# One kernel, one change: the head's order of work, and where three modulation rows are computed

## The chip, the cores and the metric

The kernel runs on one core of a Trainium2 chip. A core has TensorE (matrix products, PE in the profile; PEld is its loading of stationary operands), VectorE (DVE), ScalarE (ACT), GpSimd (POOL) and SyncE (SP), which here does nothing but issue transfers between the chip's memory and the core's. The metric is the device time of one execution in microseconds (us).

## What is computed

One layer of a hybrid backbone on 1024 tokens of 1024 features, in float32, with 256 context tokens beside them. Cut to what matters here:

```python
sh1, sc1, g1, sh2, sc2, g2 = adaln(c, ada_w, ada_b)       # silu(c) @ ada_w + ada_b, 6 rows of 1024
csh1, csc1, *_ = adaln(c_ctx, ada_w, ada_b)
h_ctx = modulate(ctx, csh1, csc1)                         # standardize(.) * (1 + scale) + shift
k_ctx, v_ctx = context_kv(h_ctx, w_in)
h = modulate(x, sh1, sc1)
u_hy, q, k, v, gates = split(h @ w_in)
y_hy = hyena_branch(u_hy)                                 # short convolution, then a long one
y_at = latent_attention(q, k, v, cos, sin, k_ctx, v_ctx, sinks)
x = layer_norm(ALPHA * x + g1 * mix(y_hy, y_at, gates))
x = layer_norm(ALPHA * x + g2 * hier_moe(modulate(x, sh2, sc2)))
```

## The kernel before

Every large product is made exact by splitting both factors into a high and a low part (`split`, lines 250 to 254: ScalarE rounds the high part, VectorE subtracts) and adding three products (`mm3`, lines 256 to 260).

**The head** is `phase_start`, with the queues' order written out by hand: inside `tc.manual_schedule()` the order of the program is the order on each engine. The modulation of x (shift and scale) is computed in four quarters of 256 features. `fetch(q)` (line 365) loads 2 MB of `ada_w` in two transfers into one of three `aw` buffers; `part(q)` (line 377) multiplies it with the silu of both conditions in 16 products; ScalarE copies the result to `mrow`; `turned(q)` (line 387) turns it into columns by 8 small products, and VectorE adds the bias into `ad`. `load(t)` (line 373) loads 128 tokens of x; `stat_a` and `stat_b` (lines 398 to 420) standardize them, even tiles by VectorE's statistics, odd ones by ScalarE's. `turn(q, g)` (line 457) transposes two blocks of 128 features of 512 tokens (g is the half) on TensorE and returns `then`, which applies scale and shift and splits the result into `hT` (`mod_split`, line 548: ScalarE and VectorE) and puts the two blocks on the list `todo`. `kv(n)` (line 445) takes n items off that list; each is six products, three into keys and three into values. `later` holds the weights of keys and values (`wri`, `wv`), loaded early and split at `run(x)`. Last come the context's statistics, `context(k)` for four pairs of blocks, and the context's keys and values; `self.ahead()` (line 608) then loads and splits the first weights of the queries. There are two split weight buffers (`whi`, `wli`) and one raw one (`wri`).

Before the change, the statistics of x0 to x3 come ahead of `part(0)`; then follow turn(0, 0), the splits of `later`, the statistics of x4 to x7, and from there on quarter after quarter.

**The query stage** is `phase_qkv`. Keys are rotated and split, values turned, then `queries()` projects four chunks of queries (48 products each) and rotates, scales and splits them on VectorE and ScalarE. Outside the hand-written part a planner orders each engine's queue by its own estimate of when an instruction can start, in the order of the program where several can. `weave(...)` (line 200) interleaves generators in proportion to given counts. Here it weaves the queries with `mod_rows` (line 690) for `MOD_Q`, three half rows of the later modulation (g1, sh2): each is cleared on POOL, gets its bias by a transfer, then adds 8 loads of 128 x 512 weights (256 KB, buffers `mr`, the tile `aw` in the profile) by one VectorE operation each into `ac`, sums over the partitions by a product with ones (`p1`, the tile `p`), is copied by ScalarE and stored to `d_row`. These rows are read only much later.

**The attention stage** is `phase_att`: it weaves `attend` (66 steps, 32 blocks of scores and values) with `conv_all` (96 steps: twelve projections of 48 products for the short convolution).

Of the kernel before, what the change touches and what calls it, by code (L numbers as in the profile page):

```python
# [18 lines left out]
P = 128  # L19
# [225 lines left out]
class K:  # L245
# [106 lines left out]
    def phase_start(self):  # L352

        tc, nc, A = self.tc, self.nc, self.A
        with ExitStack() as es:
# [10 lines left out]
            def fetch(i):  # L366
                w = aw[i] = sb.tile([P, 8, 512], F32, name=f"aw{i}", tag="aw", bufs=3)
                for j in range(2):
                    c0 = j * 1024 + i * 256
                    nc.sync.dma_start(w[:, :, j * 256:(j + 1) * 256],  # L370
                                      A["ada_w"][:, c0:c0 + 256].rearrange("(k p) c -> p k c", p=P))
# [5 lines left out]
            def part(i):  # L377

                pm[i] = ps.tile([P, 512], F32, name="pm", tag="pm", bufs=1)
                for r in range(2):  # L380
                    for j in range(4):
                        k = 4 * r + j
                        nc.tensor.matmul(pm[i][32 * j:32 * j + 32], s2[:, k], aw[i][:, k], start=(r == 0), stop=(r == 1))
                mrow[i] = sb.tile([P, 512], F32, name="mrow", tag="mrow", bufs=2)
                nc.scalar.activation(mrow[i], pm.pop(i), AF.Copy)
# [69 lines left out]
            def turn(q, g):  # L455

                pt = [block(k, g) for k in (2 * q, 2 * q + 1)]

                def then():
                    for k in range(2):  # L460
                        out(2 * q + k, g, pt[k])
                        todo.append((2 * q + k, g))
                return then

            with tc.manual_schedule():
                for t in range(4):
                    load(t)
                fetch(0)
                wv, jk = (self.kvp.tile([P, 1280], F32, name=n, tag="kvb") for n in ("wv", "jk"))
                jk = jk[:, :1024]  # L470
                later = [self.ahead(True), self.ahead(True, wv)]
                for t in range(4, 8):
                    load(t)
                for i in range(1, 3):
                    fetch(i)
                nc.vector.memset(s2, 0.0)
                nc.scalar.activation(s2[:, :, :2], cols[:, :16].rearrange("p (k c) -> p k c", c=2), AF.Silu)
                warm = sb.tile([P, 1], F32, name="warm", bufs=1)
                nc.scalar.activation(warm, self.eps, AF.Sqrt)
                nc.vector.tensor_copy(silc, s2[:, :, 0])  # L480
                for c in range(2):
                    nc.vector.tensor_copy(bias[:, :8, c], cols[:, 16:24])
                    nc.vector.tensor_scalar(bias[:, 8:, c], cols[:, 24:32], 1.0, None, op0=OP.add)
                stat_a(xn[0], 0)
                stat_a(xn[1], 1)
                stat_b(xn[0], 0)
                stat_a(xn[2], 2)
                stat_b(xn[1], 1)
                stat_a(xn[3], 3)
                stat_b(xn[2], 2)  # L490
                stat_b(xn[3], 3)
                part(0)
                fetch(3)
                turned(0)
                turn(0, 0)()
                for x in later:
                    run(x)
                    w.append(self.w_ready.pop(0))
                stat_a(xn[4], 4)
                stat_a(xn[5], 5)  # L500
                stat_b(xn[4], 4)
                stat_a(xn[6], 6)
                stat_b(xn[5], 5)
                stat_a(xn[7], 7)
                stat_b(xn[6], 6)
                stat_b(xn[7], 7)
                kv(2)
                turn(0, 1)()
                for q in range(1, 4):
                    kv(1)  # L510
                    part(q)
                    if q == 1:
                        cx = sb.tile([P, 8, 512], F32, name="cx", tag="aw", bufs=3)
                        for t in range(2):
                            cn[t] = cx[:, 2 * t:2 * t + 2].rearrange("p a b -> p (a b)")
                            nc.sync.dma_start(cn[t], A["ctx"][t * P:(t + 1) * P])
                    kv(1)
                    turned(q)
                    then = turn(q, 0)
                    if q > 1:  # L520
                        kv(1)
                    then()
                    if q == 3:
                        for t in range(2):
                            stat_a(cn[t], t, cx[:, 4:6].rearrange("p a b -> p (a b)"))
                            stat_b(cn[t], t)
                    if q > 1:
                        kv(1)
                    turn(q, 1)()
                kv(2)  # L530
                context(0)
                kv(2)
                context(1)
                kb, vb = (self.kvp.tile([P, 1280], F32, name=n, tag="kvb") for n in ("kb", "vb"))
                for g in range(2):
                    for j, b in enumerate((kb, vb)):
                        nc.scalar.activation(b[:, g * 512:(g + 1) * 512], acc[j, g], AF.Copy)
                    context(2 + g)
            for j, b in enumerate((kb, vb)):
                pc = self.pjp.tile([P, 512], F32, name="pjc", tag="pj", bufs=4)  # L540
                for k in range(KD):
                    self.mm3(pc[:, :256], w[j][0][:, k], w[j][1][:, k], self.cT[0][k // 2][:, k % 2],
                             self.cT[1][k // 2][:, k % 2], k == 0, k == KD - 1)
                nc.scalar.activation(b[:, 1024:], pc[:, :256], AF.Copy)
                if j == 0:
                    self.ahead()
            return kb, vb

    def mod_split(self, sb, pt, ad, k, c, hi, lo):
# [89 lines left out]
    def phase_qkv(self, cps, kb, vb):  # L639
        tc, nc, A = self.tc, self.nc, self.A  # L640
        with ExitStack() as es:
# [43 lines left out]
                        nc.vector.scalar_tensor_tensor(q[oth], qb[own], 0.125, q[own].bitcast(F32), op0=OP.mult,  # L685
                                                       op1=OP.subtract)

            T2 = lambda n: sb.tile([P, 2, 256], F32, name=n, tag="mr", bufs=5)
            weave((queries(), 32), (self.mod_rows(self.pjp, T2, dict(tag="pj", bufs=4), MOD_Q), 1 + 9 * len(MOD_Q)))

    def mod_rows(self, pp, T2, ptag, parts):

# [55 lines left out]
    def phase_att(self):  # L748
        tc, nc, A = self.tc, self.nc, self.A
        with ExitStack() as es:  # L750
            sb = es.enter_context(tc.tile_pool(name="at_sb", bufs=2, reuse_waits="tile"))
            pp = es.enter_context(tc.tile_pool(name="at_ps", bufs=2, space=PSUM, reuse_waits="tile"))
            mk = sb.tile([P, 1920], BF16, name="mk", bufs=1)
            nc.gpsimd.dma_start(mk, A["k_mask"])

            def fill():
                yield from self.conv_all(pp, sb)

            weave((self.attend(pp, sb, mk), 66), (fill(), 96))

    def attend(self, pp, sb, mk):
        nc = self.nc
# [1043 lines left out]
```

## Time and profile before

| | us |
|---|---|
| median of 3 runs | 1266.92 |
| lowest, highest | 1261.25, 1267.8 |
| the profiled execution | 1266.46 |
| its span in the trace | 1264.9 |

The profile is of one execution. All later rows and times within it are counted from the start of its span, and 1.56 us of its time lie outside the span. Busy time is the time in which an engine executes an instruction that counts as work; a row of a timeline gives start, duration, engine, line and operation, the tile written and the tiles read, a count where equal neighbours are merged, and in brackets how long the engine had been idle and what it waited for.

### The profile page before, as it was taken

Reading aid. Unit: us, or ns where it says so; the run is one execution under the profiler, and the core shown is the slowest. Engines: PE = TensorE matmul, PEld = TensorE weight load, DVE = VectorE, ACT = ScalarE, POOL = GpSimd, SP = SyncE. Lnnn points to the kernel's source line nnn. Section 1 sums busy time; section 2 is a strip of 40 time slices with the busy share of each in tenths; the row PEclk is TensorE's granted clock in tenths of the full one; section 3 lists DMA queues with packets and bytes.
Section 4 is the critical chain, followed back from the end, with each engine's and each line's share of the span. In section 5 each row is a group of like instructions: output and inputs, shape, how many; then the busy total and the mean of one; then the engine's idle time right before and its main releaser. Section 6 shows DMA issues by size and latency. Waiting matters only on the chain. (4 is left out here: it accounts for less than half of the span.)

```text
span 1264.9 us, 16231 instructions
## 1 busy us (share of the span) xinstructions
PE 1122.6 (89%) x5640; PEld 901.4 (71%) x5640; DVE 925.7 (73%) x1715; ACT 600.0 (47%) x1023; POOL 149.1 (12%) x159
## 2 busy tenths in 40 slices
PE   3788799999999999998998879899977999999970
PEld 2576588888887777876887757678854777778850
DVE  4459779888887357896778777756875788878827
ACT  4464366665556444443344324323443656555505
POOL 0000000000000012122010000000313332233220
PEclk9899899999999999999998999989978999999995
DMA  9424321111111545545855588743395999999726
GB/s 330 158 71 146 102 50 63 42 59 43 59 42 62 173 158 166 171 135 179 286 154 161 164 290 280 241 156 117 80 176 205 346 335 306 300 310 320 213 42 266
DMA packets 78088, 220.07 MB, mean 174 GB/s; under 512 B 9911, under 2 KB 22839, under 8 KB 71477
## 3 DMA queue, kind: packets, MB, share of 16 engines
q1 hardware_dynamic: 64933, 180.66, 42.5%
q0 software_dynamic: 12640, 38.15, 11.2%
q8 instruction: 45, 0.74, 0.2%
q14 instruction: 38, 0.31, 0.1%
q10 hardware_dynamic: 432, 0.21, 0.1%
HBM read 178.41 MB, written 45.78 MB: 177 GB/s over the span
## 5 line engine op out<-in xcount | busy, mean ns | idle before, releaser
L258 PE MATMUL pj<-hT,whi 128*128 128x512 f32 x512 | 209.8, 410 | 4.5 <-ACT o L723 2.3
L260 PE MATMUL pj<-hT,wli 128*128 128x512 f32 x512 | 203.3, 398 | 1.6 <-DVE wli L254 1.6
L259 PE MATMUL pj<-hT,whi 128*128 128x512 f32 x512 | 204.4, 399 | 0.0
L253 ACT ACTIVATE eh<-er 128x1024 fp32r<-128x1024 f32 x96 | 99.3, 1058 | 57.9 <-PE pg L260 22.9
L254 DVE TENSOR_TENSOR el<-er,eh 128x1024 fp32r<-128x1024 f32 x96 | 113.8, 1218 | 13.7 <-ACT eh L253 13.4
L258 PEld LDWEIGHTS pj<-hT,whi 128*128 128x128 f32 x512 | 97.4, 190 | 29.2 <-issue 7.2
L260 PEld LDWEIGHTS pj<-hT,wli 128*128 128x128 f32 x512 | 97.3, 190 | 21.3 <-DVE wli L254 2.3
L259 PEld LDWEIGHTS pj<-hT,whi 128*128 128x128 f32 x512 | 97.3, 190 | 19.1 <-issue 3.4
L258 PE MATMUL pg<-eh,xh 128*128 128x512 f32 x200 | 81.1, 406 | 0.0
L259 PE MATMUL pg<-el,xh 128*128 128x512 f32 x200 | 79.3, 397 | 0.0
L260 PE MATMUL pg<-eh,xl 128*128 128x512 f32 x200 | 79.2, 396 | 0.0
L819 ACT ACTIVATE th<-pt 128x512 fp32r<-128x512 f32 (+1 forms) x88 | 44.2, 536 | 41.5 <-PE pt L815 39.6
L1545 POOL DMA_INDIRECT d_r<-y,idi x25 | 45.7, 1828 | 142.6 <-DVE y L1696 40.9
L702 DVE SCALAR_TENSOR_TENSOR ac<-aw,silc,ac 128x512 f32<-128x512 f32 x48 | 36.2, 757 | 35.5 <-DMA aw<-ada_w 35.1
L788 DVE CUSTOM_DVE_ANT_0 p<-sp,mk,srow 128x640 f32<-128x640 f32 (+1 forms) x64 | 52.8, 845 | 8.0 <-PE sp L777 6.6
L793 ACT ACTIVATE p<-p,m 128x640 f32<-128x640 f32 (+1 forms) x64 | 50.8, 797 | 15.9 <-DVE m L790 15.9
L820 DVE TENSOR_TENSOR tl<-pt,th 128x512 fp32r<-128x512 f32 (+1 forms) x88 | 52.4, 611 | 7.5 <-ACT th L819 7.4
L258 PE MATMUL po<-wo,mg 128*128 128x512 f32 x128 | 52.6, 411 | 5.4 <-DVE gt L1225 3.1
L253 ACT ACTIVATE whi<-wri 128x1024 fp32r<-128x1024 f32 x33 | 35.0, 1061 | 44.9 <-PE pj L259 32.2
L260 PE MATMUL po<-wo,mg 128*128 128x512 f32 x128 | 52.1, 407 | 0.0
L259 PE MATMUL po<-wo,mg 128*128 128x512 f32 x128 | 52.1, 407 | 0.0
L254 DVE TENSOR_TENSOR wli<-wri,whi 128x1024 fp32r<-128x1024 f32 x33 | 40.3, 1220 | 15.7 <-ACT whi L253 15.5
(476 smaller groups left out, 2768.2 us busy)
## 6 DMA issues: line engine op xcount, KB each, us to landing
er<-w_gu SPq DMA_DIRECT2D x32, 1024.0 KB, 8.3
wri<-w_in SPq DMA_DIRECT2D x33, 512.0 KB, 3.7
er<-w_dn SPq DMA_DIRECT2D x16, 1024.0 KB, 8.3
aw<-ada_w SPq DMA_DIRECT2D x48, 256.0 KB, 4.2
x<-x SPq DMA_DIRECT2D x16, 512.0 KB, 8.8
aw<-ada_w SPq DMA_DIRECT2D x8, 1024.0 KB, 12.0
d_gate<-go SPq DMA_DIRECT2D x32, 256.0 KB, 2.4
gt<-d_gate SPq DMA_DIRECT2D x32, 256.0 KB, 4.1
```

The costliest lines, as they stand in the source:

```text
L253: a = self.nc.scalar.activation(hi, src, AF.Copy)
L254: return a, self.nc.vector.tensor_sub(lo, src, hi.bitcast(F32))
L258: mm(ps, whi, xhi, start=first, stop=False)
L259: mm(ps, whi, xlo, start=False, stop=False)
L260: mm(ps, wlo, xhi, start=False, stop=last)
L702: nc.vector.scalar_tensor_tensor(acc, w, self.silc[:, k:k + 1], acc, op0=OP.mult, op1=OP.add)
L788: nc.vector.tensor_tensor_reduce(p[:, a, :T], src, mk[:, o:o + T], 1.0, self.sink[:, h0 + a:h0 + a + 1], OP.add, OP.max, m[:, a:a + 1])
L793: nc.scalar.activation(p[:, a, :T], p[:, a, :T], AF.Exp, bias=m[:, 2 + a:3 + a], accum_out=m[:, 6 + a:7 + a])
L819: nc.scalar.activation(th[:, :N], pt[:, :N], AF.Copy)
L820: nc.vector.tensor_sub(tl[:, :N], pt[:, :N], th[:, :N].bitcast(F32))
L1545: self.nc.gpsimd.indirect_dma_start(out=self.d_r, out_offset=bass.IndirectOffsetOnAxis(ap=idx, axis=0), in_=y, in_offset=None, bounds_chec ...
```

## The change

In the head, `fetch(0)` goes ahead of the first four loads of x, and `fetch(1)` between the key and value weights and the other four. `part(0)` and `turned(0)` come ahead of all statistics. The first half of the tokens (g = 0) goes through the quarters 0 and 1 before the statistics of the second half, with the splits of `later` and items of `kv` put between `turn` and `then`; afterwards the halves follow in another order, the context's statistics come behind the last `turn`, and the first weights of the queries are asked for right after the context's load. `mod_rows` for `MOD_Q` leaves the weave with the queries and joins the one of the attention, with three `mr` buffers in place of five and two `pj` banks in place of four.

```diff
             with tc.manual_schedule():
+                fetch(0)
                 for t in range(4):
                     load(t)
-                fetch(0)
                 wv, jk = (self.kvp.tile([P, 1280], F32, name=n, tag="kvb") for n in ("wv", "jk"))
                 jk = jk[:, :1024]
                 later = [self.ahead(True), self.ahead(True, wv)]
+                fetch(1)
                 for t in range(4, 8):
                     load(t)
-                for i in range(1, 3):
-                    fetch(i)
+                fetch(2)
...
+                part(0)
+                fetch(3)
+                turned(0)
                 stat_a(xn[0], 0)
                 stat_a(xn[1], 1)
...
-                part(0)
-                fetch(3)
-                turned(0)
-                turn(0, 0)()
-                for x in later:
-                    run(x)
-                    w.append(self.w_ready.pop(0))
+                then = turn(0, 0)
+                run(later[0])
+                w.append(self.w_ready.pop(0))
+                then()
+                run(later[1])
+                w.append(self.w_ready.pop(0))
+                part(1)
+                cx = sb.tile([P, 8, 512], F32, name="cx", tag="aw", bufs=3)
+                for t in range(2):
+                    cn[t] = cx[:, 2 * t:2 * t + 2].rearrange("p a b -> p (a b)")
+                    nc.sync.dma_start(cn[t], A["ctx"][t * P:(t + 1) * P])
+                wq = self.ahead(True)
+                kv(1)
+                turned(1)
+                then = turn(1, 0)
+                kv(1)
+                then()
                 stat_a(xn[4], 4)
...
                 kv(2)
                 turn(0, 1)()
-                for q in range(1, 4):
-                    kv(1)
-                    part(q)
-                    if q == 1:
...
-                    kv(1)
-                    turned(q)
-                    then = turn(q, 0)
-                    if q > 1:
-                        kv(1)
-                    then()
-                    if q == 3:
-                        for t in range(2):
-                            stat_a(cn[t], t, cx[:, 4:6].rearrange("p a b -> p (a b)"))
-                            stat_b(cn[t], t)
-                    if q > 1:
-                        kv(1)
-                    turn(q, 1)()
+                part(2)
+                turn(1, 1)()
+                kv(2)
+                turned(2)
+                turn(2, 0)()
+                kv(2)
+                turn(2, 1)()
+                kv(2)
+                part(3)
+                kv(1)
+                turned(3)
+                turn(3, 0)()
+                kv(1)
+                turn(3, 1)()
+                for t in range(2):
+                    stat_a(cn[t], t, cx[:, 4:6].rearrange("p a b -> p (a b)"))
+                    stat_b(cn[t], t)
                 kv(2)
                 context(0)
...
                 if j == 0:
-                    self.ahead()
+                    run(wq)
...
-            T2 = lambda n: sb.tile([P, 2, 256], F32, name=n, tag="mr", bufs=5)
-            weave((queries(), 32), (self.mod_rows(self.pjp, T2, dict(tag="pj", bufs=4), MOD_Q), 1 + 9 * len(MOD_Q)))
+            run(queries())
...
-            weave((self.attend(pp, sb, mk), 66), (fill(), 96))
+            T2 = lambda n: sb.tile([P, 2, 256], F32, name=n, tag="mr", bufs=3)
+            weave((self.attend(pp, sb, mk), 66), (fill(), 96),
+                  (self.mod_rows(pp, T2, dict(tag="pj", bufs=2), MOD_Q), 1 + 9 * len(MOD_Q)))
```

## Rows read from the trace of the kernel before

**Rows 1.** The page, part 1: busy time, share of the span, instructions.
```profile
PE 1122.6 (89%) x5640; PEld 901.4 (71%) x5640; DVE 925.7 (73%) x1715; ACT 600.0 (47%) x1023; POOL 149.1 (12%) x159
```

**Rows 2.** Windows by stage: stretch, its length, busy per engine, PEclk, DMA share, GB/s.
```profile
53.00:84.00 31.00, 27.47 (x164) 20.16 (x162) 14.72 (x32) 16.73 (x29) 0.52 (x1) 1.00 0.00 1
...
91.00:135.00 44.00, 32.81 (x132) 23.97 (x130) 42.15 (x46) 17.87 (x23) 1.05 (x2) 0.92 0.48 150
135.00:165.00 30.00, 28.59 (x118) 21.88 (x118) 21.22 (x23) 9.09 (x11) 0.73 (x1) 0.94 0.36 101
165.00:410.00 245.00, 240.95 (x1406) 204.67 (x1405) 206.54 (x513) 154.40 (x342) 2.24 (x25) 1.00 0.16 50
```

**Rows 3.** Windows of 2 us in the head, the same columns.
```profile
40.00:42.00 2.00, 1.32 (x5) 0.48 (x3) 0.81 (x2) 1.83 (x3) 0.00 (x0) 0.50 1.10 367
...
46.00:48.00 2.00, 2.00 (x16) 0.93 (x9) 0.00 (x0) 0.60 (x1) 0.00 (x0) 0.93 0.00 0
```

**Rows 4.** Timeline of SP in the head: start, duration, what is issued.
```profile
11.27 1.87 SPq L375 DMA_DIRECT2D x<-x  x4
...
33.76 2.87 SPq L598 DMA_DIRECT2D wri<-w_in  x1
47.27 0.82 SPq L516 DMA_DIRECT2D cx<-ctx  x2
```

**Rows 5.** Timeline of the head, all engines: statistics, first part, column, transposes.
```profile
8.73 1.28 DVE L411 BATCH_NORM_STATS2 bs<-x 128x6 f32<-128x512 f32 x2
...
16.81 3.64 PE L383 MATMUL pm<-aw,s 128*32 128x512 f32 x16 [16.81 <-DMA aw<-ada_w]
...
23.06 0.23 DVE L396 TENSOR_TENSOR ad<-pc,adb 128x4 f32<-128x4 f32 x2 [4.69 <-PE pc L393]
...
29.51 1.28 DVE L411 BATCH_NORM_STATS2 bs<-x 128x6 f32<-128x512 f32 x2
...
38.33 0.81 DVE L420 TENSOR_SCALAR x<-x,va 128x1024 f32<-128x1024 f32 x1
...
39.20 1.33 PE L425 MATMUL pt<-small,x 128*128 128x128 f32 x5 [1.25 <-DVE x L420]
...
44.37 2.83 PE L383 MATMUL pm<-aw,s 128*32 128x512 f32 x16
```

**Rows 6.** Timeline of TensorE in the head: products of 512 columns.
```profile
30.38 0.63 PE L258 MATMUL kv<-hT,whi 128*128 128x512 f32 x1
...
60.03 0.39 PE L258 MATMUL kv<-hT,whi 128*128 128x512 f32 x1
60.26 0.40 PE L259 MATMUL kv<-hT,whi 128*128 128x512 f32 x1
```

**Rows 7.** Timeline: the context's statistics and transposes, the first query product.
```profile
72.55 1.28 DVE L411 BATCH_NORM_STATS2 bs<-cx 128x6 f32<-128x512 f32 x2
...
78.61 0.66 PE L437 MATMUL pt<-small,cx 128*128 128x128 f32 x4 [2.53 <-ACT hT L557]
...
91.36 0.49 PE L258 MATMUL pj<-hT,whi 128*128 128x512 f32 x1
```

**Rows 8.** Timeline of the query stage: TensorE's waits, a VectorE addition.
```profile
107.26 0.50 PE L260 MATMUL pj<-hT,wli 128*128 128x512 f32 x1 [1.59 <-DVE wli L254]
...
115.19 1.02 PE L705 MATMUL p<-ac,onec 128*1 128x512 f32 x2 [1.07 <-DVE ac L702]
...
133.05 2.20 DVE L702 SCALAR_TENSOR_TENSOR ac<-aw,silc,ac 128x512 f32<-128x512 f32 x3
...
133.90 1.86 PE L705 MATMUL p<-ac,onec 128*1 128x512 f32 x2 [6.55 <-issue]
```

**Rows 9.** Groups, 91 to 156 us: count, busy, mean ns, idle before.
```profile
L702 DVE SCALAR_TENSOR_TENSOR ac<-aw,silc,ac 128x512 f32<-128x512 f32 x24 | 17.8, 751 | 5.3 <-DMA aw<-ada_w 4.8
...
L705 PE MATMUL p<-ac,onec 128*1 128x512 f32 x6 | 3.9, 738 | 7.6 <-issue 6.5 <-DVE ac L702 1.1
```

**Rows 10.** Waits, 165 to 412 us: who waited for whom, us, times, longest.
```profile
DVE m L795 <- ACT m L794: 12.3, 13, 1.8
```

More of the change, by code (lines that the diff above doesn't have):

```diff
@@ L508, in phase_start @@
                 turn(0, 1)()
-                for q in range(1, 4):
-                    kv(1)
-                    part(q)
-                    if q == 1:
-                        cx = sb.tile([P, 8, 512], F32, name="cx", tag="aw", bufs=3)
-                        for t in range(2):
-                            cn[t] = cx[:, 2 * t:2 * t + 2].rearrange("p a b -> p (a b)")
-                            nc.sync.dma_start(cn[t], A["ctx"][t * P:(t + 1) * P])
-                    kv(1)
-                    turned(q)
-                    then = turn(q, 0)
-                    if q > 1:
-                        kv(1)
-                    then()
-                    if q == 3:
-                        for t in range(2):
-                            stat_a(cn[t], t, cx[:, 4:6].rearrange("p a b -> p (a b)"))
-                            stat_b(cn[t], t)
-                    if q > 1:
-                        kv(1)
-                    turn(q, 1)()
+                part(2)
[15 more added lines that the diff above has]
+                    stat_b(cn[t], t)
                 kv(2)
```

## The prediction, made before the changed kernel was run

> **What bounds the kernel now.** I read the page's first part, then the table by stage, then the order of time in the head. Over the span TensorE is busy 89% and VectorE 73% [rows 1], but that is a mean over stages with different limits. [Rows 2] are the stages that the change touches. The **head** (0 to 91 us) is first bound by transfers: the DMA share is 1.10 up to about 42 us, and at 46 nothing flows [rows 3]. After that TensorE works through what is left, 27.5 of 31 us busy. In the **query stage** (91 to 156) VectorE is the bound: 42.15 of 44 us busy, TensorE only 32.8. The **attention stage** (165 to 410) is TensorE's: 240.95 of 245 us, VectorE 206.5. So the order of the head decides when the queries start (91.36, [rows 7]), VectorE decides how long they take, and what is added to the attention is paid where TensorE or VectorE has no room.
>
> The clock has two levels: a product of 512 columns takes 0.63 us early and 0.39 later, when the next starts 0.23 us on [rows 6]. I call 0.23 the high rate and 0.43 the low one. TensorE's whole head, counted in high-rate work, is about 48 us.
>
> **The head, first half.** Engines run their queues in program order here. Evidence: VectorE stands idle for 4.69 us ahead of the modulation column at 23.06, and only afterwards begins x4 at 29.51 [rows 5], though x4 to x7 were issued from 11.27 on [rows 4]. So I play the new order with old durations.
>
> (a) The weights fetch(0) go ahead of x0 to x3. Before, part(0) began at 16.81 [rows 5] with 4.4 MB landed, half of it x. With that half behind it, from the first bytes at about 2 us, I estimate 9.4 plus 1.5 for what is in flight beside it: 11. The column `ad` came 6.25 us after part(0) began and takes 0.3: 17.5.
>
> (b) turned(0) now stands before the statistics on VectorE. They began at 8.73 and now wait for `ad`: 17.5, or 8.8 later, although x0 is there at about 12.5. The chain took 9.6 us, so x3 is ready at 27.2 and the first transposes end at 28.4, as 39.20 + 1.33 follows x7 [rows 5].
>
> (c) TensorE goes on, where it used to wait: part(1) 2.83 [rows 5], one kv item of six products 2.6 at the low rate, turned(1) 1.0, turn(1,0) 1.2, another kv item. ScalarE and VectorE finish turn(1,0)'s output at 38.5, and only then, in program order, come the statistics of x4 to x7. They took 9.6 us from 29.51 (x7 ends at 38.33 + 0.81, [rows 5]); now 38.5 to 48.1, so 9.0 later. In exchange TensorE has done 6.5 us of high-rate work by then that used to follow (part(1) 1.9, turned(1) and turn(1,0) 0.95 each, two kv items 2.7). Balance: +2.5.
>
> **The head, second half.** From the end of turn(0,1)'s transposes (39.20 + 1.33 = 40.5, [rows 5]) to the queries took 50.9 us for 40.9 us of work; 10 were lost to the low rate, which ended shortly after 46 [rows 3], and to waits. Now 34.4 us of work start at 49.4. Low rate until about 55: 2.5 us, since TensorE idles from 41 to 48 as it did from 33 to 41. After that a kv pair (2.7 us) stands beside every output of ScalarE (2.1 us), so the small waits go. One wait grows. The context's statistics come behind turn(3,1). Their chain took 5.7 us (72.55 to 78.3; transposes at 78.61, [rows 7]); it would begin at about 74.3, and only one kv pair, ending at 75.0, covers it. TensorE idles 5 us instead of 2.5. From the context's transposes on it is 12.75 us as before (78.61 to 91.36), 2.4 of them lost. Sum: 49.4 + 34.4 + 2.5 + 5 + 2.4 = 93.7 against 91.36, about **+2**. Bounds: -4, if the weights land at 9.5 and the high rate is kept; +6, if the clock falls in both new gaps.
>
> That gap of 5 us has two nearest rows: one of 2.5 us (76.1 to 78.6) left the rate high, one of 6.55 us ahead of 133.90 left the next products low [rows 8]. I charge nothing for it in the sum and 2.4 us (12 products at 0.43 for 0.23) in the upper bound. The Trainium skill (TensorE: Matmul & The Clock Gate, "HAM oscillation — how this bites in real kernels") speaks against such gaps: an array left waiting is throttled again and starts each burst cold. By that rule the head would be +4.4 instead of +2, and the time 1262.4.
>
> The early request for Q's weights I cost at nothing: the third `wri` was already issued at 33.76 [rows 4], and its split waits for a free weight buffer at 90.07, which the change leaves where it is. Without that cover it would be one transfer, 3.5 us. The context's load, at 47.27 before, moves to about 42, with 30 us to spare [rows 4].
>
> **The query stage loses the three rows.** That removes 24 VectorE operations, 17.8 us [rows 9], the 24 loads of 256 KB between Q's weight loads on SP, and three products `p1`. `p1` cost 3.9 us busy and 7.6 idle on TensorE [rows 9], most of it one wait: 6.55 us ahead of 133.90, where the last addition on VectorE started at 133.05 [rows 8]. After it six products ran at the low rate: 1.2 us. The stall at the second chunk stays: 107.26 waits for `wli`, which stands behind the four `kk` operations on VectorE; three additions (2.2 us) stood ahead of those, but ScalarE's `kk` and `whi` end late as well, so only 0.8 goes. Sum 3.9 + 7.6 + 1.2 + 0.8 = **-13.5**. Then TensorE's 192 products at 0.23 are the bound and VectorE, with about 9 us a chunk against 10.9, keeps up. Bounds: -9, if part of the additions is issued ahead into this stage (its buffers are free then); -17, if the `kk` stall goes as well.
>
> **The attention stage gets them.** TensorE: three `p1` of 1.02 us [rows 8] in a stage that is 98% busy: 3.1. `p1` takes one of two `pj` banks, so the next group of the convolution waits for the copy-out of the last (two ScalarE operations, about 1.4 us) unless attention products stand between: 0.5 each, 1.5. VectorE: 18 us more on 206.5 gives 225 of 245. It now waits 12.3 us for ScalarE's sums alone [rows 10], and additions are ready at any time, so they fall into such holes: 0.4. Queued behind an addition that waits for its load are scores and values, and TensorE after them; with three `mr` buffers, one the sum, two loads are ahead, at a step of 9 us against some 4 to land. Of the rows' other steps POOL's three clearings of the sum take 0.53 us each, on an engine that does nothing there but clear two columns a chunk. On SP a load that waits for a buffer holds back `d_at` and the next weights, which have 4 us to spare. Sum **+5**. Bounds: 0 (the 4 us that TensorE idles cover it; less is excluded, since work is added to the bound) and +21 (18 + 3.1, nothing hidden).
>
> The rest, from 410 us on, has the same instructions and moves as a whole. +2 - 13.5 + 5 = -6.5 on the profiled execution's 1266.46 gives **1260.0**; the median of 1266.92 is 0.46 above that, inside the spread of the three runs.
>
> **Rivals.**
> 1. *The rows slip back.* Their buffers lie outside the query stage's, so the planner may start them there. Then part of VectorE's load stays: query stage -6, attention +2, head +2: 1264.5. For it: other steps far down the program are already issued early. Against: `p1` has no bank before the attention, so at most one row can be finished. Chance 0.18.
> 2. *The head gains.* Statistics of x4 to x7 begin when x has landed, near 30, not at 38.5, because columns or outputs come sooner than I play them. Then the 6.5 us that were done ahead count in full and the queries start near 85: 1251.5. Against: the idle VectorE at 18.4 to 23 [rows 5]. Chance 0.18.
> 3. *Slower: VectorE becomes the attention's bound.* Convolution tails come in bursts there (two operations of 1.28 us and a split of 1.22 in one step); with an addition on top, VectorE lags and TensorE waits at every one. Price up to 21 us: 1276. The balance tips when the attention pays 11.5, slower by 0.5% from 18. Against: 20 us of VectorE still free. Chance 0.12.
> 4. *The clock falls.* The context's gap of 5 us ends at the low rate, and the 12 products behind it cost 2.4 us more: 1262.4. For it the row of 6.55 us, against it that of 2.5 us, both above. Chance 0.08. The Trainium skill's section on HAM oscillation (TensorE: Matmul & The Clock Gate) describes the same.
>
> **How the numbers follow.** The forecast has 0.44 and lies on the edge: 0.5%, about what a measurement of this kernel can tell from no change, is 6.3 us, so faster is below 1260.6. I split it 55 to 45 between faster and no change. Faster: 0.24 + 0.18 (rival 2) + 0.03 (some of rivals 1 and 4) = 0.45; slower 0.12 (rival 3); same the remaining 0.43. The range from 1249 to 1270 takes in rivals 1, 2 and 4 and the bounds of each single term but the attention's upper one.
>
> **What would show it.** In the profile after: x4's statistics at about 38 and TensorE idle before 48; an idle of some 5 us before the context's transposes; the first query product at 92 to 95 (below 88: rival 2); no additions and no `p1` before the attention (eight or more: rival 1) and the scores about 11.5 us earlier; the attention's length up by 5, with VectorE near 92% (above 10: rival 3). The prediction is wrong if VectorE doesn't keep to program order in the head, or if TensorE's waits in the query stage have another cause than the rows.

## The result and the profile after

The kernel after takes 1249.84 us (median of 8 runs, 1239.07 to 1254.49); the kernel before, on the same chip, 1260.97 (8 runs, 1256.94 to 1267.8). The ratio, taken over all executions and not from the two medians, is 0.9894, 95% interval 0.9857 to 0.9931. Run again later on another chip, beside the kernel before there, it was 0.9881 (0.9841 to 0.9921). That is 13 to 15 us off some 1260. The prediction had 1260.0: faster by 6.5 us than its profiled execution, about half of what came.

Two tables carry the reading. First the profile after: busy time, share of the span and instructions of each engine, as in [rows 1],

```profile
PE 1116.8 (90%) x5640; PEld 897.2 (72%) x5640; DVE 923.3 (74%) x1715; ACT 599.8 (48%) x1023; POOL 150.6 (12%) x159
```

and the windows by stage, with the columns of [rows 2] (PEclk is the granted clock of TensorE as a share of the full one):

```profile
53.00:87.00 34.00, 27.81 (x147) 21.34 (x145) 14.21 (x31) 15.89 (x27) 0.00 (x0) 0.90 0.09 32
94.50:138.50 44.00, 44.00 (x197) 36.19 (x196) 38.52 (x36) 21.15 (x26) 0.00 (x0) 1.00 0.19 60
149.00:395.00 246.00, 243.98 (x1416) 204.59 (x1415) 219.46 (x536) 155.46 (x345) 4.02 (x28) 1.00 0.24 73
```

The middle row is the find: in the query stage TensorE is now busy all the time at the full clock, where [rows 2] had it busy for three quarters.

Second, five marks in every trace that was taken (read from the timelines, one execution each, in us): the first query product; from it to the first score; from that to the last attention row `y`; from that to the first argument of the Fourier filter on ScalarE; and from that to the end of the span. The experiments are told below; "rows" are the three modulation rows.

| kernel | first query | query stage | attention | step behind it | the rest |
|---|---|---|---|---|---|
| before | 91.36 | 64.79 | 250.74 | 13.13 | 844.9 |
| after | 94.54 | 44.07 | 254.94 | 10.69 | 843.5 |
| after, again | 96.08 | 44.06 | 254.84 | 10.12 | 840.4 |
| new head alone | 95.13 | 65.84 | 250.54 | 13.14 | 833.1 |
| rows moved alone | 92.71 | 44.06 | 254.93 | 10.08 | 833.5 |
| before without the rows | 91.16 | 44.06 | 250.92 | 11.51 | 834.7 |
| after without the rows | 95.00 | 44.03 | 251.22 | 11.52 | 834.8 |
| before, few additions | 89.85 | 54.72 | 250.74 | 13.12 | 847.1 |
| before, no sums | 91.28 | 49.35 | 254.52 | 11.53 | 837.2 |
| before, split first | 91.33 | 61.61 | 250.49 | 11.53 | 845.4 |
| after, late addition | 91.93 | 44.04 | 255.24 | 10.31 | 828.7 |
| after, early context | 88.72 | 44.06 | 254.91 | 9.94 | 836.8 |
| both of these | 86.70 | 44.04 | 255.19 | 10.03 | 830.6 |
| and x4 early | 83.60 | 44.05 | 255.05 | 10.12 | 840.3 |

Before against after: +3.2 in the head, -20.7 in the query stage, +4.2 in the attention, -2.4 in the step behind it: 15.7 us sooner. The last column is the same code in all kernels that compute the rows, and spreads over 18 us from one execution to the next; the unchanged kernel after had 843.5 once and 840.4 once. So the total of one profiled execution can't price a change here. The query stage and the attention can: traces with the same work there agree within 0.1 and 0.7 us. The ratio over many executions can, to some 0.4%. The first query product is less sharp: with the same head it came at 89.85 to 92.71 in six traces of the old one and at 94.54 to 96.08 in four of the new one. The new head costs 3.9 us between the means of the two groups, and 1.8 to 6.2 by single traces.

### The profile page after: what moved, and what is told of

Read it like the earlier page. It is cut to its first block, busy times and chain, and to the rows that moved or that the text cites. A ratio compares the mean times of both kernels' runs of the same rounds, so it can differ in the third digit from the quotient of the medians.

```text
span 1247.7 us, 16198 instructions
## 1 busy us (share of the span) xinstructions
PE 1116.8 (90%) x5640; PEld 897.2 (72%) x5640; DVE 923.3 (74%) x1715; ACT 599.8 (48%) x1023; POOL 150.6 (12%) x159
```

## The experiments

### Which part brings the time?

The new head alone, with the rows left beside the queries:

```diff
 (the kernel after)
-            run(queries())
+            T2 = lambda n: sb.tile([P, 2, 256], F32, name=n, tag="mr", bufs=5)
+            weave((queries(), 32), (self.mod_rows(self.pjp, T2, dict(tag="pj", bufs=4), MOD_Q), 1 + 9 * len(MOD_Q)))
```

and the attention's weave as before.

> The new order of the head alone; the three modulation rows stay beside the query products, where they were before. Theory A (the head by itself loses, and all of the gain comes from the query stage): the first query product comes at 94.5 us, as in the kernel after (94.54), 3.2 later than before (91.36); the ACT order with the splitting of Q's second weight chunk behind the keys' copies is that of the kernel before, so the scores start about 3 us later than before's 156.15, at 159 to 160, and the whole is 2 to 4 us slower than before. Theory B (the head's reordering brings a gain that the later stages show, by the filled products or by a clock that stays high): the total is 5 to 10 us faster than before with the rows still in the query stage.

Measured: ratio 1.0056 (1.0029 to 1.0082). That is theory A in kind: first query product at 95.13, first score at 160.97, one microsecond later than expected, and the whole about 7 us slower by the ratio (4.5 between the medians) where 2 to 4 were expected. The rows alone, with the old head, are the other half of the diff:

> The three modulation rows moved beside the attention, and the head left in its old order. Theory A: the first query product comes at 91.4 as before, the query stage is 18 to 20 us shorter, and the scores start near 136; the attention pays 2 to 3 us, so the whole is 13 to 16 us under before and 2 to 4 us under the kernel after. Theory B (the rows' move pays only with the new head, because that is what brings Q's second weights early): Q's second chunk still waits for its load or for its split, the scores start no earlier than 143, and the whole is 5 to 8 us under before.

Measured: ratio 0.9851 (0.9810 to 0.9892), and no stall at Q's second chunk, which is theory A in kind. Its numbers were too low: 19 us under before by the ratio, not 13 to 16, the query stage 20.7 us shorter and not 18 to 20, the attention 4.2 us longer and not 2 to 3. Against the kernel after it is 4 to 5 us by the ratios, whose intervals overlap, and 2.5 to 3.3 us up to the Fourier filter in the traces. So the head costs and the rows pay; 0.56% lost and 1.49% won leave 0.93%, where the whole change has 1.06%.

### What do the rows cost in each place?

Both kernels without the rows' computation, which prices them:

```diff
-            weave((queries(), 32), (self.mod_rows(self.pjp, T2, dict(tag="pj", bufs=4), MOD_Q), 1 + 9 * len(MOD_Q)))
+            run(queries())
+            for i in MOD_Q:
+                nc.sync.dma_start(self.d_row[i // 2:i // 2 + 1, i % 2 * 512:i % 2 * 512 + 512],
+                                  self.A["ada_b2"][:, i * 512:(i + 1) * 512])
```

> The kernel before without the computation of the three modulation rows: the product of silu(c) with ada_w for these rows is left out (the rows are stored as their bias alone), so times behind the attention are read as those of another kernel. It prices all that the rows cost in the query stage. Theory A (24 additions on VectorE, the sums over partitions and the order that the rows force on ScalarE cost together what the stage lost in the kernel after): from the first query product to the first score 44 to 46 us, where before has 64.8 and the kernel after 44.1; no stall of TensorE near 105. Theory B (the forecast's sum: sums over partitions and their clock, 13.5 us): 51 us, and the stall of 3.6 us near 105 to 107 stays.

> The kernel after without the computation of the three modulation rows (the same is left out as in the run before this one). It prices the rows in the attention. Theory A: they cost TensorE their own sums alone, 3.1 us of products and under 1 us of waits, and the stretch from the first score to the last attention row is 2 to 4 us shorter than in the kernel after (255.2 us, 138.6 to 393.8). Theory B (VectorE's 17.8 us of additions are paid too, because VectorE stands near the bound): 8 to 18 us shorter. Theory C (they lie wholly beside other work): less than 1 us.

Measured: theory A in the first, the query stage takes 44.06 us without any rows, to a hundredth what it takes with the rows moved away:

```profile
91.16:135.22 44.06, 44.06 (x197) 36.22 (x195) 38.61 (x36) 21.10 (x27) 0.00 (x0) 1.00 0.18 60
```

So the move takes out all of what they cost there, 20.7 us. The attention takes 251.2 without them and 254.9 with them, 3.7 us (theory A); over all traces it is 250.5 to 251.2 without and 254.8 to 255.2 with (the kernel whose additions trail into it, below, aside). The ratios are 0.9825 (0.9781 to 0.9869) for the kernel before without the rows and 0.9888 (0.9844 to 0.9933) for the kernel after without them. The groups of the kernel after in the attention (count, busy, mean ns, idle before) show what the 3.7 us are:

```profile
L710 DVE SCALAR_TENSOR_TENSOR ac<-aw,silc,ac 128x512 f32<-128x512 f32 x24 | 17.9, 745 | 0.8 <-DMA aw<-ada_w 0.7
...
L713 PE MATMUL p<-ac,onec 128*1 128x512 f32 x6 | 3.1, 591 | 0.7 <-DVE ac L710 0.7
```

3.1 us of sums and 0.7 of waiting for them make 3.8. The 17.9 us of additions cost nothing that can be seen: VectorE is busy for 226.10 of the stage's 254.94 us, and waits less for ScalarE than in [rows 10], 7.2 us:

```profile
DVE m L805 <- ACT m L804: 7.2, 10, 1.8
```

### Why did they cost 20.7 in the query stage?

The forecast had 13.5. First which of the rows' steps it is: keep the sums and leave out 21 of the 24 additions,

```diff
-                nc.vector.scalar_tensor_tensor(acc, w, self.silc[:, k:k + 1], acc, op0=OP.mult, op1=OP.add)
+                if parts is not MOD_Q or k == KD - 1:
+                    nc.vector.scalar_tensor_tensor(acc, w, self.silc[:, k:k + 1], acc, op0=OP.mult, op1=OP.add)
```

> The kernel before with the rows where they were, all their loads and their three sums over partitions kept, and 21 of the 24 additions on VectorE left out (only the last slice of each row is multiplied and added, so the rows are wrong values; times behind the attention are those of another kernel). In the kernel before the stretch from the first query product to the first score took 64.75 us, of which VectorE was busy 55.6 and TensorE 52.2; without any rows it took 44.1. Theory V (VectorE is what the stage is bound by; TensorE's stalls at 105, 107 and 133 are where that shows): taking away 21 additions of 0.74 us brings the stage down to 47 to 49 us, that is 44.1 and the 3.9 us of the sums' products. Theory P (the forecast's: the sums over partitions and the waits around them cost, additions do not): the waits for the sums shorten, since their last addition is there sooner, but 3.9 us of products, the stall of 3.6 us at the keys' copies and a fallen clock stay, and the stage takes 52 us or more.

or keep the additions and leave out the sums:

```diff
-            p1 = pp.tile([1, 512], F32, name="p1", **ptag)
-            nc.tensor.matmul(p1, self.onec, acc, start=True, stop=True)
-            nc.scalar.activation(acc[0:1], p1, AF.Identity, bias=1.0 if i // 2 == 2 else 0.0)
+            if parts is not MOD_Q:
+                p1 = pp.tile([1, 512], F32, name="p1", **ptag)
+                ...
```

> The kernel before with the rows' 24 additions kept where they were and the three sums over partitions and their copies left out (so the rows are wrong values). Theory V (VectorE bounds the stage): TensorE stands nowhere for a sum, but the query chunks' own VectorE work is still queued behind additions, so the stage takes 54 to 60 us where before took 64.75, and the stall at 105 to 107 stays at 3.6 us. Theory P (the sums are what cost): 64.75 less 3.9 of products, 7.6 of waits and 1.2 of low clock, about 52 us.

Measured: 54.72 us without the additions (ratio 0.9923, 0.9889 to 0.9957), 49.35 without the sums (0.9901, 0.9868 to 0.9933). Theory V, that VectorE's load is what the stage is bound by, falls twice. Additions without sums cost the stage 5.3 us, although VectorE stays at 48.56 of 49.35:

```profile
91.28:140.63 49.35, 46.25 (x197) 37.20 (x196) 48.56 (x54) 19.22 (x25) 1.05 (x2) 0.97 0.51 168
```

The 5.3 us are 3.1 of the stall at the second chunk (2.0 and 1.1) and 2.2 of low clock (46.25 busy less 44.06). Four of the 24 additions, and the end of the last chunk's own work on VectorE, then trail behind the first score, and that attention is 254.52 instead of 250.7. From the first query product to the last attention row the kernels take 303.9 without the sums and 305.5 without the additions, where before takes 315.5 and no rows 295.0: the sums are worth 11.7 us and the 21 additions 10.1. These two don't add up to the whole of 20.5, though they come near it: the 7.6 us of waiting for the sums go in both kernels, and the stall at the second chunk stays in both. Theory P had expected about 52 us without the sums, 2.7 too many.

What theory P had right in the other kernel: additions cost by making the sums late (the wait for the sums goes, 7.6 us), and with almost none of them

```profile
89.85:144.57 54.72, 49.92 (x203) 37.01 (x201) 41.39 (x40) 24.15 (x31) 1.05 (x2) 0.97 0.47 156
```

is the 44.06 with 3.1 of sums, 2.8 of low clock and 4.8 of waits. The stall at the second chunk is still there, and so is a third wait that the prediction had not counted, ahead of the scores:

```profile
PE pj L258 <- ACT whi L253: 1.8, 1, 1.8
PE pj L260 <- DVE wli L254: 1.6, 1, 1.6
PE sp L778 <- ACT qb L679: 1.4, 1, 1.4
```

The stall hangs on an order on ScalarE. In the kernel before (first two lines) the keys' four copies `kk` stand ahead of the split of Q's second weights; in the kernel after (the others) the split stands ahead of them, as soon as the weights land:

```profile
98.66 5.15 ACT L662 ACTIVATE kk<-kb 64x1280 fp32r<-64x1280 f32 x4
103.83 1.06 ACT L253 ACTIVATE whi<-wri 128x1024 fp32r<-128x1024 f32 x1
```

```profile
99.30 1.06 ACT L253 ACTIVATE whi<-wri 128x1024 fp32r<-128x1024 f32 x1 [2.07 <-DMA wri<-w_in]
...
101.68 2.56 ACT L671 ACTIVATE kk<-kb 64x1280 fp32r<-64x1280 f32 x2
```

The planner made that order, and not the edits of the head: with the new head alone ScalarE has `kk` at 102.42 and the split at 107.59, with the rows moved alone the split at 97.44 and `kk` at 99.84. The split is late in every trace whose query stage holds the rows' loads, with few additions and without sums too, unless it is forced. What in those loads turns the planner was not tried. Forced it was, with the rows in place:

```diff
             rotate(kb)
+            self.ahead()
+            self.early = True
             for v in range(2):
 ...
-            if g == 0:
+            if g == 0 and not self.early:
                 self.ahead()
+            elif g == 0:
+                self.early = False
```

> The kernel before with the rows where they were, and Q's second weight chunk asked for and split ahead of the keys' copies, which are what the split stood behind before (in the kernel after, the split stands ahead of them). Theory V (VectorE bounds the stage): the stall of 2.0 and 1.6 us at 105 to 107 goes, and TensorE waits by as much longer for the sum at 134, since the last addition comes no sooner: the stage stays within 1.5 us of 64.75. Theory K (the stall is a cost of its own, lost by the order alone): the stage is 4 to 6 us shorter, 59 to 61 us.

Measured: 61.61 us, 3.2 less, between the two theories; the ratio of 0.9967 (0.9933 to 1.0001) can't be told from no change.

```profile
91.33:152.94 61.61, 49.64 (x204) 36.79 (x202) 55.21 (x61) 24.38 (x31) 1.05 (x2) 0.92 0.46 146
```

The stall of 3.6 us is gone and TensorE waits as much longer for the sum, 10.56 us where [rows 8, 9] had 7.6 in two pieces:

```profile
118.92 1.87 PE L709 MATMUL p<-ac,onec 128*1 128x512 f32 x2 [10.56 <-DVE ac L706]
```

So in waits theory V was right: 3.6 less against 3.0 more. The rest of what is won is the clock. TensorE's busy time of a stage, less the 44.06 that the products take at the full clock and less the sums, is taken as what the low one costs (the first products behind a wait, 0.50 us instead of 0.39, are in it): before 52.20 - 44.06 - 3.9 = 4.2 us, here 49.64 - 44.06 - 3.9 = 1.7. Before had a run of products at the low clock behind each of two stalls; this is the first of them:

```profile
107.26 0.50 PE L260 MATMUL pj<-hT,wli 128*128 128x512 f32 x1 [1.59 <-DVE wli L254]
...
108.78 0.63 PE L258 MATMUL pj<-hT,whi 128*128 128x512 f32 x1
109.20 0.63 PE L259 MATMUL pj<-hT,whi 128*128 128x512 f32 x1
...
111.24 0.39 PE L258 MATMUL pj<-hT,whi 128*128 128x512 f32 x1
```

### What does the new head lose, and can it be had back?

The rows of the kernel after that answer to [rows 5, 7]: VectorE's wait for the column, the statistics of x0 and of x4, the context's transposes and the first query product.

```profile
17.47 0.23 DVE L396 TENSOR_TENSOR ad<-pc,adb 128x4 f32<-128x4 f32 x2 [8.42 <-PE pc L393]
17.62 1.27 DVE L411 BATCH_NORM_STATS2 bs<-x 128x6 f32<-128x512 f32 x2
...
37.48 1.28 DVE L411 BATCH_NORM_STATS2 bs<-x 128x6 f32<-128x512 f32 x2
...
47.17 1.33 PE L425 MATMUL pt<-small,x 128*128 128x128 f32 x5 [1.25 <-DVE x L420]
48.43 3.09 PE L383 MATMUL pm<-aw,s 128*32 128x512 f32 x16
...
76.79 0.30 PE L437 MATMUL pt<-small,cx 128*128 128x128 f32 x1 [2.96 <-DVE cx L420]
79.53 0.90 PE L437 MATMUL pt<-small,cx 128*128 128x128 f32 x3 [2.44 <-DVE cx L420]
...
80.65 0.63 PE L259 MATMUL kv<-hT,whi 128*128 128x512 f32 x1
```

Two stalls can be read from them: VectorE stands 8.42 us at an addition, about 4.9 of them with x0 landed (it came at 12.58 in the next kernel), and TensorE stands 5.4 us ahead of the context's transposes, with the low clock behind it. Each was taken away alone. The waiting addition goes behind the statistics of x0 to x3:

```diff
                 part(0)
                 fetch(3)
-                turned(0)
                 stat_a(xn[0], 0)
 ...
                 stat_b(xn[3], 3)
+                turned(0)
                 then = turn(0, 0)
```

> The kernel after with VectorE's addition that waits for the first modulation quarter moved behind the statistics of the first four token tiles. In the kernel after the statistics begin at 17.6, as VectorE stands 8.4 us at that addition. Theory A (that wait is what the new head loses): the statistics run while the quarter is summed and turned, the fourth tile is ready at about 21 instead of 27.2, the first transposes end near 24, and all that follows comes 3 to 5 us sooner, the first query product at 90 to 91.5 instead of 94.5. Theory B (the load of the tokens or of the weights is late next, and the gain goes there): less than 1.5 us.

Measured: the statistics begin when x0 lands, and the first transposes end at 24.7 instead of 28.6:

```profile
12.58 1.29 DVE L411 BATCH_NORM_STATS2 bs<-x 128x6 f32<-128x512 f32 x2 [3.79 <-DMA x<-x]
...
23.36 1.32 PE L425 MATMUL pt<-small,x 128*128 128x128 f32 x5 [1.25 <-DVE x L420]
```

3.9 us won there, of which 3.0 are left at the statistics of x4 (34.48 instead of 37.48) and 2.6 at the first query product (2.6 to 4.1 against the four traces of the new head): short of theory A, well over B. The ratio is 0.9864 (0.9820 to 0.9908). On the way part(1) took 3.24 us instead of 2.79 and waited 0.44 for its weights. Then the context's statistics one step of products ahead:

```diff
                 turn(2, 1)()
+                for t in range(2):
+                    stat_a(cn[t], t, cx[:, 4:6].rearrange("p a b -> p (a b)"))
+                    stat_b(cn[t], t)
                 kv(2)
 ...
                 turn(3, 1)()
-                for t in range(2):
-                    ...
```

> The kernel after with the context's statistics moved one step of key and value products ahead, so that VectorE and ScalarE do them while TensorE has products. In the kernel after TensorE stands 5.4 us ahead of the context's transposes, and the 12 products behind them took 0.63 us instead of 0.39, at the lower of the two clock levels. Theory A (both come from the place of the statistics): the wait goes and the clock stays high, 5.4 us and 12 times 0.24 = 2.9 us, less up to 3 us where VectorE's output of the third quarter is now behind the statistics; the first query product comes at 86 to 90 instead of 94.5. Theory B (the third quarter's outputs are late by as much): 93 or later.

Measured: first query product at 88.72, ratio 0.9842 (0.9811 to 0.9874), theory A. The transposes and the products behind them run without a wait at the full clock; the price is 1.9 us for the third quarter's copy, as ScalarE is in the context's statistics until 68.43, when it begins it:

```profile
76.09 0.60 PE L437 MATMUL pt<-small,cx 128*128 128x128 f32 x4
...
76.76 0.39 PE L259 MATMUL kv<-hT,whi 128*128 128x512 f32 x1
```

```profile
PE pc L393 <- ACT mrow L385: 2.6, 2, 1.9
```

Both together, and on top of it the statistics of x4 ahead of part(1) (its `stat_a` and `stat_b` move from behind turn(1, 0) to behind the second split), next to the kernel after, unchanged, on the same chip:

> The kernel after, unchanged, beside the three that follow. The stage times of its first trace should come again to within 0.7 us: first query product at 94.5 to 95.2, first score 44.1 later, last attention row 254.9 after that. What lies behind the first Fourier stage took 843.5 us in its first trace and 829 to 847 us in other kernels with the same code there. Theory A (that spread belongs to the execution and not to the kernel): it comes out elsewhere within 829 to 847 this time. Theory B (the head's order fixes it): 843 to 844 again.

> Both repairs of the new head together: the waiting addition behind the statistics of the first four tiles, which alone brought the first query product to 91.9, and the context's statistics ahead. Theory A (two stalls in different places add up): 2.6 us earlier than with the second repair alone, 84 to 87.5; the query stage, attention and the step behind them as in the kernel after, so 8 to 10 us under it. Theory B (the load of the context or of the weights is late next): no more than the better of the two alone.

> As the run before this, and with the statistics of the fifth token tile moved ahead of the second quarter's sum, into the 2.5 us in which VectorE stands before it. Theory A: ScalarE begins the sixth tile's squares about 2.7 us sooner, and the second half's transposes end 2 to 3 us sooner, so the first query product comes 2 to 3 us sooner than in the run before this. Theory B (the fifth tile has not landed by then, or the second quarter's modulation is put off by as much): 0.5 us or less.

Measured: 86.70 and 83.60, theory A in both by the first query product; the two repairs add up with a loss of half a microsecond, and x4 brings 3.1. The second step from 88.72 to 86.70 is no more than the same head differs by between executions, and the ratio of both, 0.9843 (0.9801 to 0.9884), is that of the early context alone. What shows it is TensorE's wait for standardized tokens in the head, which falls at each step. For the kernel after (the same with the early context), both repairs and x4 early:

```profile
PE pt L425 <- DVE x L420: 15.2, 8, 4.2
```

```profile
PE pt L425 <- DVE x L420: 12.2, 8, 2.3
```

```profile
PE pt L425 <- DVE x L420: 7.8, 7, 1.8
```

The medians of this comparison are 1258.16 before, 1243.49 after (again), 1237.13 with the early context, 1234.97 with both and **1231.62** with x4 early, 0.9794 of before (0.9756 to 0.9832). That interval lies under the one of the kernel after, 0.9841 to 0.9921: this is the version that beats both before and after. It overlaps with that of the rows moved alone (0.9810 to 0.9892), so that the repaired head beats the old one is shown by the first query product, 83.60 against 89.85 to 92.71, and not by the total. The kernel after, again, had its rest at 840.4, not at 843.5: theory A there too. Its first query product missed the range that was expected, 96.08 and not 94.5 to 95.2.

## Why the prediction was right or wrong

**The head: right in its order, and 0.8 to 2.4 us short at the end, near by luck.** Played forward, it had part(0) at 11, the column at 17.5, x3 ready at 27.2, transposes done at 28.4, x4's statistics at 38.5, those of x7 done at 48.1, the context's at 74.3. The trace has 11.22, 17.47, 27.2 (26.43 + 0.81), 28.6, 37.48, 47.1, 73.75. The gap ahead of the context's transposes was to be 5 us and is 5.4. What it took for the less likely case happened: behind that gap the clock was low, 12 products in 5.1 us instead of 2.7, at a granted clock of 0.52 of the full one, the lower of its two levels (1.2 and 2.4 GHz). That is rival 4's mechanism, with its price of 2.4 us. By the rule of the Trainium skill named there (TensorE: Matmul & The Clock Gate, "HAM oscillation — how this bites in real kernels") the burst behind such a gap starts cold; this row agrees with it. The two traces of the kernel after have the first query product at 94.54 and 96.08, against 93.7 forecast. In the first, two errors offset that price: the statistics were done 1.0 us sooner than played, and the low rate behind them, played until about 55 for 2.5 us, ended near 51 (granted clock 0.54 from 49 to 51, 1.00 from 51 to 53), about half of it. In the second, 5 products were slow, and the 2.7 us had been lost ahead of the gap, part of them by part(1) (3.64 us instead of 2.79); that 93.7 + 2.4 meets 96.08 is chance.

**Rival 2** (the head gains) had asked for statistics at 30. They came at 37.48 and the head alone is slower, 1.0056. The early x4 shows what it would have needed: with the statistics free of the columns that they don't read, x4's begin at 28.68, and with the context's moved as well the queries at 83.60.

**The query stage: the failed term.** The forecast's four pieces were sums 3.9, waits for them 7.6, low clock 1.2, stall at the second chunk 0.8. The trace of before itself gives 12.6 us of waits (64.79 less 52.20 busy) and 8.1 of busy time over the 44.06:

```profile
91.36:156.15 64.79, 52.20 (x203) 37.98 (x202) 55.60 (x61) 24.49 (x31) 1.05 (x2) 0.92 0.42 133
```

```profile
104.94 0.50 PE L258 MATMUL pj<-hT,whi 128*128 128x512 f32 x1 [1.98 <-ACT whi L253]
...
156.15 1.21 PE L777 MATMUL sp<-kk,qs 128*128 128x256 f32 x8 [1.41 <-ACT qb L679]
```

These are sums 3.9, waits for them 7.6, stall 3.6 (1.98 here and the 1.59 of [rows 8]), the wait ahead of the scores 1.4, low clock 4.2, together 20.7. So the forecast left 7.2 us in the stage that did not stay there: 2.8 of the stall, 1.4 of the third wait and 3.0 of the low clock, of which it had counted one run of slow products and not the other. Two were counting errors that a look at the whole stage would have caught: its busy and idle time at the full clock could have been set against the 192 products at 0.23, which the text itself named as the new bound: they are 44.2, and 64.8 - 44.2 is 20.6. The third is the sentence "the stall at the second chunk stays", with "ScalarE's `kk` and `whi` end late as well": it took the planner's order on ScalarE as given, and the order changed when the rows' loads were gone. The bound of -17 named that stall, and no bound named the rest. Why the wait ahead of the scores goes with the rows stays open.

The prediction also called VectorE the bound of that stage, at 42.15 of 44 us busy. It was full, and yet its load alone did not set the end: without the sums, with 20 of the 24 additions still done in it, the stage fell to 49.35, and 3.1 of the 5.3 us left above 44.06 are the stall, which is one of order. TensorE's own queue made the additions urgent, as the sums stood in it between query products.

**The attention: right.** +5 forecast, 4.2 measured (3.7 against its own kernel without rows), in the forecast's pieces: sums 3.1 as forecast, waits 0.7 instead of 1.5 and 0.4. VectorE is at 89% there, and rival 3 (slower, VectorE the bound) did not come: it was to show as over 10 us.

**Rival 1** (rows slip back) did not come: POOL, VectorE and TensorE do nothing of the rows in the query stage, whose VectorE time is 38.59 us with the rows moved and 38.61 without any.

**The rest "moves as a whole": 2.4 us off.** In the step behind the attention the kernel before waits for a bank (first line), and the clock falls behind it (0.57 granted from 408 to 412). With the rows in the attention that wait is gone in every trace; one of 0.7 to 1.5 us for a load stands there further on. Why the banks fall out that way was not tried.

```profile
407.46 0.50 PE L258 MATMUL pj<-hT,whi 128*128 128x512 f32 x1 [2.25 <-ACT o L723]
...
408.84 0.63 PE L259 MATMUL pj<-hT,whi 128*128 128x512 f32 x1
```

**The base.** The forecast was set against the profiled execution, 1266.46, with the remark that the three runs' median is as high (0.46 above it). Later medians of the kernel before are 1260.97, 1257.78, 1261.05 and 1258.16. Of the 10.2 us between 1260.0 and 1249.84, 5.5 are that (1266.46 - 1260.97); the other 4.7 are the terms (-11.1 between the medians against -6.5). By the stages of the two traces the change is -15.7: against the forecast the head is 1.2 worse, the query stage 7.2 better, the attention 0.8 better and the step behind it 2.4 better.

## What to carry to other kernels

When work leaves a stage, price it from the other end as well: what the stage takes if the engine that is left as its bound runs without a stop, and not only the stalls whose cause is plain. An engine that is nearly always busy need not be the bound: look for the instruction on the critical engine that makes its work urgent, here the three sums. And work that needs nothing from a wait should stand ahead of it in its queue: here three moves that put statistics ahead of a wait brought the first query product from 94.54 to 83.60.

## What the runs showed of the hardware that was not expected

The same wait of 2.25 us ended in different clocks. In the kernel before it is followed by products of 0.63 us (above); in the same place of the kernel without rows by products of 0.39:

```profile
386.71 0.50 PE L258 MATMUL pj<-hT,whi 128*128 128x512 f32 x1 [2.26 <-ACT o L725]
...
388.20 0.39 PE L258 MATMUL pj<-hT,whi 128*128 128x512 f32 x1
388.43 0.39 PE L259 MATMUL pj<-hT,whi 128*128 128x512 f32 x1
```

The step behind the attention follows it: 13.1 us where the clock fell (before, new head alone, few additions), 11.5 where it did not (no rows in either kernel, no sums, split first). Nor is the price of one gap fixed: behind the same two waits of 2.96 and 2.44 us ahead of the context's transposes, the kernel after ran 12 products at or near the low clock in its first trace and 5 in its second. What decides between them stays open. Open too is what makes the last 840 us of the kernel differ between 828.7 and 847.1 from execution to execution, with the same instructions. TensorE's busy time for the same 3627 products there is 743.1 us in the shortest and 753.5 in the longest, so 10 of the 18 us are slower products and 8 are waits.
